# Two of the four token tiles of the dilated heads' v are accumulated in the retention's PSUM banks

## The chip, the cores and the metric

The kernel runs on one core of a Trainium2 chip, as one launch. The metric is the device time of one execution in microseconds. A core has five engines that run side by side, each through its own list of instructions in a fixed order: PE (matrix products, with the loads of its weights, PEld, beside them), DVE, ACT and POOL (element by element work) and SP, which here only issues DMAs. Matrix products are accumulated in PSUM, which has eight banks of 128 x 512 fp32; before a bank can take the next product, what stands in it has to be read out ("evacuated") by ACT or DVE.

## The reference

Two layers on 512 tokens of width 1024, in fp32. Each layer adds to x an attention part with three kinds of heads that all come from one projection of the normalised x, and then an MLP with squared relu. Cut to what matters:

```
def hybrid_layer(x, ...):
    h = rms_norm(x, attn_norm_w)
    ret_cols, dsa_cols, dil_cols = split(h @ w_in)
    mixed = concat([retention_mixer(ret_cols),    # 4 heads, chunks of 128, gated
                    dsa_mixer(dsa_cols),          # 4 heads, each query sees its 128 best keys
                    dilated_mixer(dil_cols)])     # 8 heads, three patterns of window and stride
    x = x + mixed @ w_out
    h = rms_norm(x, mlp_norm_w)
    return x + square(relu(h @ w_up)) @ w_down

def dsa_mixer(cols):
    q, c_kv, q_idx, k_idx, w_idx = split(cols)
    # the indexer: 8 small heads score all keys, and the 128 best of each query are kept
    logits = einsum('bqhd,bsd->bqhs', q_idx, k_idx)
    score = einsum('bqhs,bqh->bqs', relu(logits), w_idx)
    idx = top_k(where(causal, score, -inf), 128)
    return softmax(q . k[idx]) . v[idx]

def dilated_mixer(cols):
    q, k, v = split(cols)          # 8 heads of 64 columns each
    outs = [dilated_branch(q, k, v, window, dilation) for window, dilation in DIL_PATTERNS]
    return sum(softmax(lses) * outs)
```

The change is about v of the dilated heads: h times 512 columns of w_in.

## The kernel before

**Products.** Every fp32 operand is split into two halves of a rounded format, hi and lo, and every product is made of three matmuls (hi hi, hi lo, lo hi). A projection over 1024 rows is thus a group of 24 matmuls into one PSUM bank. `wform` (L336) puts weight columns on the partitions and all 512 tokens along the row (128x512); `tform` (L348) puts 128 tokens on the partitions and the columns along the row (128x256 for v). The splits of the weights ("w" in the rows) are made by ACT (hi, L278) and by POOL or DVE (lo, L286), some groups ahead.

**PSUM.** The eight banks are three pools: `mm` with 2 banks for the projections, `at` with 4 for attention scores and their products, and `rt` with 2. The `rt` banks are used by the retention, in the second half of a layer's attention, and by the down projection of the MLP. A pool gives its banks in turn, so a group of matmuls in `mm` starts only when the group two before it has been evacuated. A name such as mm_163_839 in the rows is the 839th tile to be made, of pool `mm`.

**The attention of a layer.** It begins with the stages of `ORD`, 'tv idx top dv0':

- tv: token parts (retention's v, the latent and the indexer's keys).
- idx, the indexer: for each pair of its 8 heads a projection of q, evacuated by ACT (L420) and DVE (L421); scores on PE into `at` (L443 and L444); a relu on ACT (L586) into a buffer P; a weighted sum on DVE (L591). A mask follows (L593).
- top: 16 rounds of MAX (L602) and MATCH_REPLACE (L603) on DVE, on three score tiles (512, 384 and 256 wide) each, and then the bias (L607).
- dv0: `dil_v` for heads 0 to 3. For each of 4 token tiles t, 24 matmuls of 128x256 (L348), and `evac_v`: a copy of the bank on ACT (L520), a hi cast of it on ACT (L524), and the subtraction for lo on POOL (L526), which reads the copy and not the bank.

Then come the heads, with "fill" work beside them: the projections q (L423 on ACT, L424 on DVE) and k (L436 on ACT, L438 on DVE) of further heads, `dil_v` for heads 4 to 7 (dv1, fill 'd'), the gates (L644 on ACT, L645 on DVE), the retention's q and k (L620, L623), and the retention itself (L657 to L733). A softmax head needs transposes on PE (L352), their copies by ACT (L485) and DVE (L486), and products with v (L491). At the end mixed @ w_out is added to x (L828).

**What sets the order.** The code is recorded once, and a scheduler (`schedule_with_timeline_sim=True`) then sets the order of each engine's instructions, by a simulated timeline and by the priorities of the table `PR`. So a stage later in the code can stand ahead of an earlier one: it depends on when the scheduler holds its operands and its bank to be free. On the chip each engine runs its list strictly in that order, and waits where an operand or a bank isn't there.

Of the kernel before, what the change touches and what calls it, by code (L numbers as in the profile page):

```python
# [123 lines left out]
class Kern:  # L124
# [412 lines left out]
    def dil_v(self, L, act, g):  # L537
        us = [(self.unit((L, "dv", g, k)), (k, k + 1, k + 2, k + 3)) for k in (0, 4)]
        for t in range(NT):
            ps = self.mm()  # L540
            self.tform(us, act, t, ps, 256)
            self.evac_dil(ps[:, 0:256], g, t)
        self.done(2)
# [586 lines left out]
```

## Time and profile before

| | us |
|---|---|
| median of 3 runs | 1255.89 (1255.29 to 1259.02) |
| the profiled execution | 1252.02 |
| its span in the trace | 1250.0 |
| attention of layer 0, about | 20 to 301 |
| MLP of layer 0, about | 301 to 620 |
| attention of layer 1, about | 635 to 915 |

The rows below come from the trace of that one execution; times in them count from the start of the span. Layer 1 repeats layer 0 some 615 us later. In the windows, "busy" of PE counts a matmul up to its modelled end, and PEld is the load of weights, which lies beside the matmuls. An idle time in a timeline stands in brackets behind the instruction that ended it, with the instruction that released it. PEclk is the granted clock of PE: 1.00 is 2.4 GHz, 0.5 is 1.2 GHz.

### The profile page before, as it was taken

How to read it: one execution, taken by the hardware profiler on the slowest of the kernel's cores; microseconds unless marked ns; L12 is line 12 of the kernel's file. 1: busy time of each engine (PE TensorE's matmuls, PEld its weight loads, DVE VectorE, ACT ScalarE, POOL GpSimd, SP SyncE). 2: the span in 40 equal slices, each digit the busy share in tenths (PEclk: the TensorE clock that was granted, in tenths of full speed). 3: DMA queues.
4: the chain of work that ended last, by engine and by line, in shares of the span. 5: the costliest groups of instructions: out<-in, count | busy, mean ns of one | idle time of the engine just before them, and what ended most of it. 6: DMA issues, size and time to landing. Idle time of an engine off the chain costs nothing.

```text
span 1250.0 us, 16890 instructions
## 1 busy us (share of the span) xinstructions
PE 1216.8 (97%) x6116; PEld 1031.2 (82%) x6116; DVE 915.4 (73%) x1582; ACT 680.1 (54%) x1241; POOL 474.7 (38%) x461
## 2 busy tenths in 40 slices
PE   7999999989999999999999999999899999999997
PEld 5987888878888888888889888878798888888886
DVE  6599757856785875857866996586769759577596
ACT  6646658734644535445556466586465445454454
POOL 3443648543411403204224545665534032041232
PEclk9999999999999999999999999999999999999999
DMA  7423223224435052151054332241170531514301
GB/s 214 119 72 106 68 69 119 69 67 120 150 103 152 16 186 84 64 171 31 21 164 114 93 84 85 69 124 45 51 250 21 183 87 56 180 35 135 84 1 68
DMA packets 142180, 122.73 MB, mean 98 GB/s; under 512 B 6801, under 2 KB 114065, under 8 KB 142098
## 3 DMA queue, kind: packets, MB, share of 16 engines
q1 hardware_dynamic: 140178, 118.52, 31.5%
q10 hardware_dynamic: 1920, 3.15, 1.0%
q8 instruction: 48, 0.79, 0.3%
q14 instruction: 34, 0.28, 0.1%
HBM read 114.31 MB, written 4.19 MB: 95 GB/s over the span
## 4 chain that ended last, share of the span: by engine, by line
PE 83%; DVE 13%; ACT 2%; issue 1%; DMA 0%; SPq 0%; POOL 0%; POOLq 0%; DVEq 0%; ACTq 0%
PE mm L336 34%; PE mm L348 15%; PE rt L1036 14%; PE at L1036 7%; DVE sc L603 3%; PE mm L1036 3%; DVE top L602 3%; PE at L352 2%; PE at L491 2%; PE at L443 1%; PE at L444 1%; PE at L336 1%; DVE ph L462 1%; PE rt L690 1%; DVE Q L424 1%
## 5 line engine op out<-in xcount | busy, mean ns | idle before, releaser
L336 PE MATMUL mm<-act,w 128*128 128x512 f32 (+2 forms) x2352 | 514.5, 377 | 1.4 <-DVE Q L424 1.4
L336 PEld LDWEIGHTS mm<-act,w 128*128 128x128 f32 x2352 | 424.2, 188 | 78.3 <-PE at L352 1.8
L286 POOL TENSOR_TENSOR w<-raw,w 128x512 fp32r<-128x512 f32 (+1 forms) x124 | 159.6, 1310 | 85.0 <-ACT w L278 70.0
L278 ACT CAST w<-raw 128x1024 fp32r<-128x1024 f32 (+1 forms) x138 | 142.8, 1037 | 81.2 <-PE rt L1036 27.6
L1036 PE MATMUL rt<-w,U 128*128 128x512 f32 x768 | 183.2, 389 | 0.0
L286 DVE TENSOR_TENSOR w<-rd,w 128x1024 fp32r<-128x1024 f32 x112 | 144.8, 1304 | 50.0 <-ACT w L278 50.0
L286 DVE TENSOR_TENSOR w<-raw,w 128x1024 fp32r<-128x1024 f32 (+1 forms) x76 | 94.4, 1243 | 106.2 <-ACT w L278 105.9
L1036 PEld LDWEIGHTS rt<-w,U 128*128 128x128 f32 x768 | 144.2, 188 | 29.9
L993 POOL TENSOR_TENSOR st<-s 128x256 f32<-128x256 f32 x32 | 39.1, 1222 | 330.1 <-ACT s L982 325.3
L278 ACT CAST w<-rd 128x1024 fp32r<-128x1024 f32 x112 | 117.6, 1050 | 83.4 <-PE rt L1036 41.7
L348 PE MATMUL mm<-w,act 128*128 128x256 f32 (+2 forms) x768 | 142.7, 336 | 5.6 <-ACT xv L524 3.1
L348 PEld LDWEIGHTS mm<-w,act 128*128 128x128 f32 x768 | 119.4, 191 | 18.7 <-ACT xv L524 3.6
L348 PE MATMUL mm<-w,mix 128*128 128x512 f32 x384 | 99.4, 406 | 1.6 <-DVE Q L424 1.1
L1036 PE MATMUL at<-w,U 128*128 128x512 f32 (+1 forms) x396 | 97.7, 386 | 0.0
L304 DVE TENSOR_TENSOR rd<-rd,rd 128x1024 f32<-128x1024 f32 x64 | 94.3, 1473 | 0.6
L1036 PEld LDWEIGHTS at<-w,U 128*128 128x128 f32 x396 | 73.6, 188 | 15.0
L348 PEld LDWEIGHTS mm<-w,mix 128*128 128x128 f32 x384 | 71.5, 193 | 16.3 <-PE rt L352 1.5
L980 ACT ACTIVATE s<-mm 128x512 f32<-128x512 f32 x62 | 36.9, 595 | 84.8 <-PE mm L336 75.1
L997 ACT CAST U<-st 128x1024 fp32r<-128x1024 f32 x32 | 33.7, 1054 | 80.9 <-POOL st L994 80.9
L991 POOL TENSOR_TENSOR st<-s,s 128x256 f32<-128x256 f32 x32 | 36.6, 1145 | 92.0 <-ACT s L982 92.0
L998 DVE TENSOR_TENSOR U<-s,U 128x256 fp32r<-128x256 f32 x64 | 63.8, 997 | 0.0
L463 ACT ACTIVATE ph<-ph,sm 128x128 f32<-128x128 f32 (+1 forms) x96 | 53.9, 562 | 16.8 <-DVE sm L462 16.0
(165 smaller groups left out, 1712.6 us busy)
## 6 DMA issues: line engine op xcount, KB each, us to landing
raw<-in_w_up_dram SPq DMA_DIRECT2D x64, 512.0 KB, 4.4
rd<-in_w_down_dram SPq DMA_DIRECT2D x32, 1024.0 KB, 5.1
raw<-in_w_in_dram SPq DMA_DIRECT2D x48, 512.0 KB, 3.9
raw<-in_w_out_dram SPq DMA_DIRECT2D x16, 512.0 KB, 3.8
xv<-in_x_dram SPq DMA_DIRECT2D x7, 512.0 KB, 4.9
KH<-KH ACTq DMA_DIRECT2D x24, 128.0 KB, 2.3
raw<-in_w_in_dram SPq DMA_DIRECT2D x8, 256.0 KB, 2.9
xd<-xv SPq DMA_DIRECT2D x4, 512.0 KB, 3.1
```

What stands on the lines that cost most here:

```text
L278: self.nc.scalar.copy(hi, src)
L286: eng.tensor_tensor(lo[:, i:i + step], src[:, i:i + step], hi[:, i:i + step].bitcast(F32), op=ALU.subtract)
L304: sub = lambda o, a, b: self.nc.vector.tensor_tensor(o, a, b, op=ALU.subtract)
L336: self.nc.tensor.matmul(ps[:cols, toks[0]:toks[1]], a, b, start=(k == 0 and j == 0), stop=(k == KB - 1 and j == 2))
L348: self.nc.tensor.matmul(ps[:, :w], a, b, start=(n == 0), stop=(n == tot - 1))
L463: nc.scalar.activation(p, p, AF.Exp, bias=a, scale=-1.0, accum_out=b)
L602: nc.vector.max(m, sc[b])
L603: nc.vector.match_replace(sc[b], m, sc[b], SENT)
L980: nc.scalar.activation(s, ps, AF.Relu)
L993: tt(st[:, 2], a[:, 0], a[:, 1], op=ALU.subtract)
L998: nc.vector.tensor_tensor(lo, src, hi.bitcast(F32), op=ALU.subtract)
L1036: nc.tensor.matmul(ps[:, c0:c1], a, w, start=(new and n == 0), stop=(n == 11), skip_group_check=True)
```

## The change

In `dil_v`, token tiles 0 and 1 still go to `mm` and tiles 2 and 3 go to `rt`. `dil_v` is called twice in each layer, as dv0 and as dv1. No instruction is added or removed.

```diff
--- before.py
+++ after.py
@@ -537,7 +537,7 @@
     def dil_v(self, L, act, g):
         us = [(self.unit((L, "dv", g, k)), (k, k + 1, k + 2, k + 3)) for k in (0, 4)]
         for t in range(NT):
-            ps = self.mm()
+            ps = self.mm() if t < 2 else self.rt_bank()
             self.tform(us, act, t, ps, 256)
             self.evac_dil(ps[:, 0:256], g, t)
         self.done(2)
```

Since the scheduler now has other banks for these tiles, it writes another order on all engines from the first attention stages of each layer to near its end; from about 280 us on, and in the MLP, the order of PE is as before. The two layers change alike.

The first place is on PE in the stage idx, at the scores at_101 of the indexer; mm_123 and mm_139 are its projections, w_78 and w_92 are the weights of dv0, mm_163/rt_163 is its tile 2 and mm_166/rt_166 its tile 3. Before:

```order
L443 MATMUL at_99_528<-KH_87_474,Q_94_511 128x256
L444 MATMUL at_99_528<-KH_87_474,Q_94_511 128x256
L443 MATMUL at_101_534<-KH_87_474,Q_94_511 128x512
L444 MATMUL at_101_534<-KH_87_474,Q_94_511 128x512
L336 MATMUL mm_123_624<-act_16_146,w_74_428 128x384 x6
L336 MATMUL mm_139_696<-act_13_143,w_76_433 128x384 x6
L336 MATMUL mm_139_696<-act_14_144,w_76_433 128x384 x6
```

And now:

```order
L443 MATMUL at_101_534<-KH_87_474,Q_94_511 128x512
L444 MATMUL at_101_534<-KH_87_474,Q_94_511 128x512
L336 MATMUL mm_123_624<-act_15_145,w_74_428 128x384 x2
L336 MATMUL mm_123_624<-act_16_146,w_74_428 128x384 x6
L348 MATMUL rt_163_839<-w_78_438,act_13_143 128x256 x3
L348 MATMUL rt_163_839<-w_78_438,act_14_144 128x256 x2
L336 MATMUL mm_139_696<-act_13_143,w_76_433 128x384 x5
L443 MATMUL at_103_540<-KH_87_474,Q_94_511 128x384
L444 MATMUL at_103_540<-KH_87_474,Q_94_511 128x384
```

Five matmuls of dv0's tile 2 now stand among the first projections and scores of the indexer, where there was none.

The second place is on PE at the indexer's last score, at_153; mm_173 is the projection of q for the first head. Before:

```order
L443 MATMUL at_153_762<-KH_87_474,Q_142_727 128x256
L444 MATMUL at_153_762<-KH_87_474,Q_142_727 128x256
L348 MATMUL mm_163_839<-w_78_438,act_13_143 128x256 x6
L348 MATMUL mm_163_839<-w_78_438,act_14_144 128x256 x6
L348 MATMUL mm_163_839<-w_92_505,act_15_145 128x256 x6
L348 MATMUL mm_163_839<-w_92_505,act_16_146 128x256 x6
L348 MATMUL mm_166_869<-w_78_438,act_13_143 128x256 x6
L348 MATMUL mm_166_869<-w_78_438,act_14_144 128x256 x6
L348 MATMUL mm_166_869<-w_92_505,act_15_145 128x256 x6
L348 MATMUL mm_166_869<-w_92_505,act_16_146 128x256 x6
L336 MATMUL mm_173_911<-act_13_143,w_108_577 128x512 x6
```

And now:

```order
L348 MATMUL mm_161_810<-w_92_505,act_16_146 128x256 x4
L443 MATMUL at_153_762<-KH_87_474,Q_142_727 128x256
L444 MATMUL at_153_762<-KH_87_474,Q_142_727 128x256
L348 MATMUL mm_161_810<-w_92_505,act_16_146 128x256
L348 MATMUL rt_166_869<-w_78_438,act_13_143 128x256 x4
L348 MATMUL rt_166_869<-w_78_438,act_14_144 128x256 x6
L348 MATMUL rt_166_869<-w_92_505,act_15_145 128x256 x6
L348 MATMUL rt_166_869<-w_92_505,act_16_146 128x256 x6
L336 MATMUL mm_173_911<-act_13_143,w_108_577 128x512 x6
```

Before, 48 of dv0's 96 matmuls stood behind the last score, in two banks of `mm`; now 73 stand ahead of it, and 22 of those behind it are in `rt`.

The third place is on DVE, in the top-k, at the evacuation of mm_173 (L424). Before:

```order
L602 MAX top3_241_1347<-sc3_90_479 128x8
L602 MAX top2_242_1350<-sc2_89_478 128x8
L602 MAX top1_243_1353<-sc1_88_477 128x8
L603 MATCH_REPLACE sc3_90_479<-top3_241_1347,sc3_90_479 128x512
L603 MATCH_REPLACE sc2_89_478<-top2_242_1350,sc2_89_478 128x384
L603 MATCH_REPLACE sc1_88_477<-top1_243_1353,sc1_88_477 128x256
L602 MAX top3_244_1356<-sc3_90_479 128x8
L424 SCALAR_TENSOR_TENSOR Q_176_942<-mm_173_911,Q_176_942 64x512
```

And now:

```order
L602 MAX top1_192_1056<-sc1_88_477 128x8
L603 MATCH_REPLACE sc2_89_478<-top2_191_1053,sc2_89_478 128x384
L603 MATCH_REPLACE sc3_90_479<-top3_238_1338,sc3_90_479 128x512
L603 MATCH_REPLACE sc1_88_477<-top1_192_1056,sc1_88_477 128x256
L602 MAX top2_239_1341<-sc2_89_478 128x8
L602 MAX top3_241_1347<-sc3_90_479 128x8
L602 MAX top1_240_1344<-sc1_88_477 128x8
L424 SCALAR_TENSOR_TENSOR Q_176_942<-mm_173_911,Q_176_942 64x512
```

Before, 13 MAX and 12 MATCH_REPLACE stood between the indexer's last sum and this evacuation; now it is 9 and 7.

The fourth place is on PE at mm_206, a projection of k; w_187 and w_199 are the weights of dv1, and rt_260 and rt_263 its tiles 2 and 3. Before:

```order
L491 MATMUL at_212_1202<-PT_214_1208,xv_159_805 128x512
L352 MATMUL at_215_1213<-cst_85,ph_181_985 128x128 x4
L352 MATMUL at_217_1225<-cst_85,ph_181_985 128x128 x2
L336 MATMUL mm_206_1162<-act_13_143,w_174_936 128x512 x6
L336 MATMUL mm_206_1162<-act_14_144,w_174_936 128x512 x6
L336 MATMUL mm_206_1162<-act_15_145,w_174_936 128x512 x6
L336 MATMUL mm_206_1162<-act_16_146,w_174_936 128x512 x5
L491 MATMUL at_212_1202<-PT_214_1208,xv_159_805 128x512
L336 MATMUL mm_206_1162<-act_16_146,w_174_936 128x512
```

And now:

```order
L491 MATMUL at_212_1202<-PT_214_1208,xv_159_805 128x512
L352 MATMUL at_215_1213<-cst_85,ph_181_985 128x128 x4
L352 MATMUL at_217_1225<-cst_85,ph_181_985 128x128 x2
L348 MATMUL rt_260_1462<-w_199_1113,act_15_145 128x256 x5
L491 MATMUL at_212_1202<-PT_214_1208,xv_159_805 128x512
L348 MATMUL rt_260_1462<-w_199_1113,act_16_146 128x256 x6
L348 MATMUL rt_263_1492<-w_199_1113,act_15_145 128x256 x5
L348 MATMUL rt_263_1492<-w_199_1113,act_16_146 128x256 x6
L336 MATMUL mm_206_1162<-act_13_143,w_174_936 128x512 x5
L491 MATMUL at_212_1202<-PT_216_1218,xv_159_805 128x384
```

48 of dv1's 96 matmuls, which stood some way behind mm_206, now stand ahead of it.

How many MAX and MATCH_REPLACE stand on DVE ahead of an instruction (of 96 in all), and its place in DVE's list, for the second of each pair of evacuations:

| instruction on DVE | before | after |
|---|---|---|
| L424 of mm_173 | 29, place 106 | 21, place 98 |
| L424 of mm_198 (the bank that mm_206 takes next) | 55, place 159 | 51, place 157 |
| L438 of mm_202 | 63, place 171 | 59, place 169 |
| L438 of mm_206 (the bank that mm_255, tile 0 of dv1, takes next) | 69, place 186 | 73, place 197 |
| L645 of mm_226 | 76, place 200 | 77, place 203 |

## Rows read from the trace of the kernel before

**Rows 1.** The page, busy times and the chain that ended last (line by engine)

```profile
PE 1216.8 (97%) x6116; PEld 1031.2 (82%) x6116; DVE 915.4 (73%) x1582; ACT 680.1 (54%) x1241; POOL 474.7 (38%) x461
...
PE 83%; DVE 13%; ACT 2%; issue 1%; DMA 0%; SPq 0%; POOL 0%; POOLq 0%; DVEq 0%; ACTq 0%
```

**Rows 2.** Windows of layer 0: us, busy us per engine, PEclk, DMA share, GB/s

```profile
60.00:73.00 13.00, 10.58 (x75) 9.56 (x73) 11.94 (x19) 8.54 (x21) 2.72 (x3) 1.00 0.16 43
...
80.00:146.00 66.00, 64.49 (x351) 55.19 (x350) 65.18 (x198) 37.63 (x79) 34.78 (x36) 1.00 0.34 93
146.00:190.00 44.00, 44.00 (x223) 36.95 (x222) 20.77 (x62) 24.06 (x53) 22.58 (x27) 1.00 0.25 72
...
276.00:284.00 8.00, 8.00 (x28) 6.81 (x27) 4.17 (x10) 1.87 (x6) 3.87 (x5) 0.57 0.00 1
```

**Rows 3.** Timeline of PE, 58 to 80: start, us, instructions [idle before, releaser]

```profile
60.42 2.86 PE L348 MATMUL mm<-w,act 128*128 128x256 f32 x22 [0.28 <-DVE Q L421]
...
65.60 0.44 PE L443 MATMUL at<-KH,Q 128*128 128x384 f32 x1 [0.57 <-ACT P L586]
...
71.12 0.28 PE L444 MATMUL at<-KH,Q 128*128 128x256 f32 x1
72.97 6.01 PE L348 MATMUL mm<-w,act 128*128 128x256 f32 x48 [1.57 <-ACT xv L524]
78.82 1.55 PE L336 MATMUL mm<-act,w 128*128 128x512 f32 x6
```

**Rows 4.** Timeline of PE, 106 to 131

```profile
109.88 0.51 PE L491 MATMUL at<-PT,xv 128*128 128x512 f32 x1 [0.27 <-ACT PT L485]
...
111.72 5.49 PE L336 MATMUL mm<-act,w 128*128 128x512 f32 x23 [0.68 <-DVE Q L424]
...
125.39 3.12 PE L348 MATMUL mm<-w,act 128*128 128x256 f32 x24
...
129.95 1.33 PE L348 MATMUL mm<-w,act 128*128 128x256 f32 x9 [0.54 <-DVE P L645]
```

**Rows 5.** Waits of PE in 632 to 920 (layer 1): total us, times, longest

```profile
PE mm L348 <- ACT xv L524: 1.6, 1, 1.6
...
PE mm L336 <- DVE Q L424: 0.7, 1, 0.7
...
PE at L443 <- ACT P L586: 0.6, 1, 0.6
PE mm L348 <- DVE P L645: 0.5, 1, 0.5
```

**Rows 6.** Chain of waits, 60 to 100: start, us, what

```profile
73.77 1.38 DVE top L602 x3
75.15 1.58 DVE sc L603 x3
```

**Rows 7.** Timeline of DVE, 69 to 75 and 116 to 126

```profile
69.61 3.55 DVE L591 SCALAR_TENSOR_TENSOR sc<-P,widx,sc 128x512 f32<-128x512 f32 x6 [0.20 <-ACT P L586]
...
123.34 0.69 DVE L438 TENSOR_TENSOR KL<-mm,KH 64x512 fp32r<-64x512 f32 x1
```

**Rows 8.** Timeline of DVE, 143 to 154

```profile
143.96 1.64 DVE L607 TENSOR_SCALAR sc<-sc 128x384 f32<-128x384 f32 x2
...
147.51 0.69 DVE L645 SCALAR_TENSOR_TENSOR P<-P,mm 128x512 f32<-128x512 f32 x1 [1.18 <-ACT P L644]
148.93 0.69 DVE L486 TENSOR_TENSOR PT<-at,PT 128x512 fp32r<-128x512 f32 x1 [0.73 <-ACT PT L485]
153.17 0.68 DVE L438 TENSOR_TENSOR KL<-mm,KH 64x512 fp32r<-64x512 f32 x1 [3.55 <-ACT KH L436]
```

**Rows 9.** Timeline of POOL, 36 to 50

```profile
42.03 5.25 POOL L286 TENSOR_TENSOR w<-raw,w 128x512 fp32r<-128x512 f32 x4 [0.35 <-ACT w L278]
```

**Rows 10.** Timeline of PE, 190 to 196

```profile
191.33 0.60 PE L352 MATMUL rt<-cst,mix 128*128 128x128 f32 x4
```

**Rows 11.** Windows of layer 1, as Rows 2

```profile
890.00:896.00 6.00, 6.00 (x33) 5.20 (x33) 3.18 (x6) 2.14 (x6) 2.82 (x4) 0.72 0.02 3
```


## The prediction

> **What bounds the kernel now.** I read the page's busy times and chain first. PE is busy 1216.8 us of the 1250.0 us span, and it carries 83% of the chain that ended last, DVE 13% [rows 1]. So time can only be won where PE waits, or where its clock is low, and the sum below goes by PE's idle time alone. DVE's 13% has to lie in one stretch, and the windows show which: from 60 to 73 us DVE is busy 11.94 of 13.00 us and PE 10.58; from 80 to 146 DVE is busy 65.18 of 66.00 and PE 64.49; from 146 to 190 PE is busy 44.00 of 44.00 and DVE 20.77 of 44 [rows 2]. The middle one is the top-k, one MAX and MATCH_REPLACE after the other (1.38 + 1.58 us for a round of all three score tiles) [rows 6]. Both engines are nearly full there, so I must ask of each PE wait that goes whether DVE lets PE run ahead.
>
> Then PE's timeline, for the single waits. In the indexer there are three: 0.28 us for DVE's Q (L421), 0.57 us for a relu (L586), and 1.57 us, just before the 48 matmuls of dv0's tiles 2 and 3, for ACT's cast xv (L524) [rows 3]. The last is the wait for a bank that the change is about: tile 2 wants the `mm` bank that tile 0 still holds, and ACT reads that one out late. Sum 0.28 + 0.57 + 1.57 = 2.42 us, and the window has 13.00 - 10.58 = 2.42 too [rows 2]. In the top-k there are three more: 0.27, 0.68 and 0.54 us, in all 1.49, for PT (L485), for Q (L424) and for the gate's product (L645) [rows 4]. Layer 1 has the same: 1.6, 0.6, 0.7 and 0.5 us by the same lines [rows 5].
>
> **The change, part by part.** Nothing is added, so each term is a wait that goes or comes. (1) *The bank.* With tiles 2 and 3 in `rt` no matmul of dv0 waits for L524 of tile 0. The two `rt` banks are idle there: the next use of them, by the retention, is at 191.33 us [rows 10], long after the evacuation of dv1 too. An L348 matmul takes (78.82 - 72.97)/48 = 0.122 us [rows 3]; I hold it to be the same into `rt`. Gain 1.57.
>
> (2) *Filler in the indexer.* 5 of dv0's matmuls now stand ahead of the third row of scores, and in all 73 instead of 48 ahead of the last score. PE's other two waits there were for a bank (L421) and for at (L586), which come at a given time of DVE and ACT; PE now comes to them later, by up to 25 x 0.122 = 3.05 us, so 0.28 and 0.57 go. The weights must be ready earlier: their lo halves on POOL run from 42.03 to 47.28 [rows 9], and the first such matmul stands at the scores of at_101, which PE comes to after that. Sum of (1) and (2): 2.42.
>
> (3) *The price of (2).* The last score comes later by 3.05 - 0.28 - 0.57 = 2.2 us at most, and with it the last sums on DVE (six of them from 69.61 on, [rows 7]) and the start of the top-k. On DVE that is a delay of 0 to 2.2 us for all that stands in the top-k, less what is moved ahead. It has room at the end: L607 ends at 143.96 + 1.64 = 145.6, and then DVE waits 1.18, 0.73 and 3.55 us for ACT [rows 8], while PE waits for nothing up to 190 [rows 2]. So the delay itself costs nothing if PE gets its banks.
>
> (4) *Waits in the top-k.* For mm_173 DVE's queue is 8 half-rounds shorter, for mm_198 and mm_202 4 each; a half-round, one MAX or MATCH_REPLACE, takes (1.38 + 1.58)/6 = 0.49 us [rows 6]. So these evacuations come 2 to 4 us earlier in the queue, which outweighs the later start of 0 to 2.2. Moreover 48 matmuls of dv1 now stand ahead of mm_206, 48 x 0.122 = 5.9 us in which PE doesn't need that bank. The waits of 0.27, 0.68 and 0.54 us go: 1.49.
>
> (5) *A new wait.* L438 of mm_206 is at place 197 of DVE instead of 186. DVE does an instruction in 65.18/198 = 0.33 us there [rows 2], so it ends 11 x 0.33 = 3.6 us later, and up to 2.2 more by (3): 123.34 + 0.69 + 3.6 = 127.6 to 129.8 us [rows 7]. The matmuls that want its bank, dv1's tile 0, began at 125.39 [rows 4]; PE now comes to them 5.9 us later by (4) and 2.42 + 0.27 + 0.68 = 3.4 us earlier by the waits gone, at 127.9. So PE waits 0 to 1.9 us. I take 0.7, near the lower end, since DVE's last sums were themselves not the last thing to wait for a score: DVE still had a backlog when the last one came, at 71.12 + 0.28, and ended the sums at 73.16 [rows 3, 7]. Queued behind that matmul is all of PE; ACT and DVE have other work then.
>
> (6) *The end of the attention.* PE's list differs there in a few places, with waits under a microsecond each. From 276 to 284 us the granted clock is 0.57, between its two levels of 1.2 and 2.4 GHz, which costs (1 - 0.57) x 8 = 3.4 us [rows 2]; in layer 1 it is 0.72 for 6 us, 1.7 us [rows 11]. It follows a thin stretch of PE that the change hardly touches. I put (6) at nothing, with bounds of -5.1 (no drop in either layer) and +5.1 (twice the drop).
>
> Sum for a layer: 2.42 + 1.49 - 0.7 = 3.2 us, for two 6.4 us. The profiled execution took 1252.02 us, 2.02 around its span, so I expect 1252.0 - 6.4 = 1245.6 for its like. It lies 3.87 under the median of the runs shown, 1255.89, against which the forecast is measured: 1255.9 - 6.4 = **1249.5 us**. Own range: both layers at their best, 2 x 3.91 = 7.8, and no clock drop, 5.1, give 1243.0; the new wait at its dearest, 2 x (3.91 - 1.9) = 4.0, and a clock drop half as long again, 2.6, give 1254.5.
>
> **The rivals.** *No change: DVE sets the pace.* From 60 to 146 us DVE is busier than PE. If PE's lead is given back at each evacuation, waits of the same sum show up at other L424 and L438 lines, and the time is 1255.9. For it: DVE's 65.18 of 66.00 us [rows 2]. Against it: DVE waits 5.46 us right after the top-k while PE waits for nothing, so the top-k ends with room [rows 8]. Beside it, the Trainium skill ("Perfetto Trace Analysis", Identifying the Most-Contended Engine) takes the engine with the highest occupancy as the one to optimise first, and judges TensorE by the busy share of its weight loads. By it DVE bounds the top-k (99% against PEld's 84%), and a change that only relieves PE brings nothing there. The Trainium skill also says that a gap which repeats on the busy engine can mean too few buffers ("Perfetto Trace Analysis", Optimization Strategy); the 1.57 us gap agrees, but comes once in a layer.
>
> The Trainium skill also has a measurement against the change: "TensorE: Matmul & The Clock Gate", HAM oscillation, tells of a kernel with its loop made contiguous to which double-buffering in PSUM gave no further gain (126.6 to 125.5 us). By that the sum would be about nothing; here the trace names a wait for a bank, which the Trainium skill doesn't show of that kernel.
>
> *Slower: the later last score is what counts.* The place is the start of the top-k, behind 25 more matmuls. If the retention's inputs, the heads' evacuations and the softmaxes all hang on DVE, its 2.2 us of delay in each layer go into the time: 1255.9 + 2 x 2.2 = 1260.3. This decides if DVE's L607 ends over 1.18 + 0.73 = 1.9 us later than now against PE's other work, so that PE waits between 146 and 160, where it has no idle time now. For it: DVE has no other slack between 60 and 146 than 0.82 + 1.06 us [rows 2]. Against it: 3.55 us of wait follow [rows 8].
>
> *The clock.* With nothing else won, a clock drop gone gives 1255.9 - 5.1 = 1250.8, one doubled 1261.0. Nothing in the rows speaks for either.
>
> **How the numbers follow.** The forecast's mechanism (waits gone, most of the lead kept) 0.60; DVE gives the pace and takes it back, 0.25; slower through the top-k, 0.15, each with the clock's play in it. 0.3% of the time, 3.8 us, is about what a measurement of this kernel can tell from no change. Of the forecast's 0.60, 0.54 lie beyond it and 0.06 within; of the 0.25, 0.19 within and 0.03 to each side; of the 0.15, 0.12 slower and 0.03 within. So faster 0.57, same 0.28, slower 0.15. The range goes from 1244, a little above the best case, to 1260, which holds the case of no change and most of the slower one.
>
> **What would show it.** Right, step by step: (1) no wait for L524 near 71 us, and L348 rows into `rt` from the first scores on; (2) PE without idle time from 60 to 80; (3) top-k starting 0 to 2.2 us after 73.77 and L607 ending by 148, with shorter DVE waits behind it; (4) no waits for L424 and L645 in the top-k; (5) one wait of under 1.9 us for L438 at an L348 into `mm`, at about 128 us; (6) a clock of about 0.57 and 0.72 at the ends of the attention. It is wrong if PE's idle sum from 60 to 146 is still near 3.9 us under other names, if PE waits between 146 and 190, or if an L348 into `rt` waits for a split of w (L286).

## The result, and the profile after

| | before | after |
|---|---|---|
| median, us | 1255.59 (1253.34 to 1259.02, 4 runs) | 1238.22 (1236.08 to 1238.82, 4 runs) |
| ratio | | 0.9854 (95%: 0.9829 to 0.9878) |
| the profiled execution, us | 1252.02 | 1236.08 |
| its span, us | 1250.0 | 1234.1 |

The kernel is 17.4 us faster by the medians, where 6.4 was forecast, and the time lies below the range of 1244 to 1260. The two profiled executions differ by 15.9 us, and that is what has to be found. The granted clock alone doesn't make it: in one series of 23 executions of before those with a mean granted clock of 0.994 to 0.996 took 1252.56 to 1255.99 us and those at 0.991 and 0.992 took 1257.06 to 1259.42, while after, at 0.994 to 0.997, took 1236.08 to 1238.82.

The page of after, to be read against [rows 1]: busy times, and the chain by engine.

```profile
PE 1207.2 (98%) x6116; PEld 1027.6 (83%) x6116; DVE 921.4 (75%) x1582; ACT 679.2 (55%) x1241; POOL 472.4 (38%) x461
...
PE 85%; DVE 12%; ACT 1%; issue 1%; DMA 1%; SPq 0%; POOL 0%; POOLq 0%; DVEq 0%; ACTq 0%
```

PE is busy for 9.6 us less, with the same 6116 matmuls, and DVE for 6.0 us more. So busy times don't tell where the time went. The windows of after, over the same stretches as [rows 2], and one of the end of layer 1's attention (us, busy us of PE, PEld, DVE, ACT, POOL with counts, PEclk, DMA share, GB/s):

```profile
60.00:73.00 13.00, 13.00 (x99) 12.64 (x98) 11.85 (x19) 8.53 (x19) 2.86 (x2) 1.00 0.16 43
...
80.00:146.00 66.00, 63.56 (x349) 54.58 (x348) 65.13 (x202) 37.97 (x80) 32.38 (x33) 1.00 0.34 94
146.00:190.00 44.00, 43.69 (x229) 37.15 (x228) 23.78 (x69) 25.98 (x57) 24.94 (x30) 1.00 0.27 78
...
276.00:284.00 8.00, 8.00 (x43) 6.65 (x42) 5.88 (x13) 3.32 (x11) 3.89 (x4) 1.00 0.00 0
...
872.00:890.00 18.00, 16.79 (x84) 14.06 (x83) 13.43 (x28) 6.80 (x19) 7.97 (x10) 0.91 0.06 19
```

From 60 to 73 us PE has no idle time left (13.00 of 13.00, it was 10.58), from 80 to 146 it has more of it than before (63.56 busy, it was 64.49). The clock drop at 276 us is gone in layer 0, and layer 1 has one of (1 - 0.91) x 18 = 1.6 us, about as before (1.7 [rows 11]). None of this makes 15.9 us. What finds it is holding the starts of the same instructions of PE against each other. These are the starts of eight groups in before: transposes in the first stage, the retention's transposes of its second, third and fourth tile, the MLP's first projection, and in layer 1 the retention's first, second and fourth tile (its first of layer 0 stands in [rows 10]):

```profile
21.51 0.60 PE L352 MATMUL at<-cst,KH 128*128 128x128 f32 x4
...
218.71 0.60 PE L352 MATMUL rt<-cst,mix 128*128 128x128 f32 x4
...
246.03 0.60 PE L352 MATMUL rt<-cst,mix 128*128 128x128 f32 x4
...
272.33 0.60 PE L352 MATMUL rt<-cst,mix 128*128 128x128 f32 x4
...
300.68 4.55 PE L336 MATMUL mm<-act,w 128*128 128x256 f32 x36
...
806.78 0.60 PE L352 MATMUL rt<-cst,mix 128*128 128x128 f32 x4
...
834.09 0.60 PE L352 MATMUL rt<-cst,mix 128*128 128x128 f32 x4
...
887.66 0.60 PE L352 MATMUL rt<-cst,mix 128*128 128x128 f32 x4
```

And in after, the same with the retention's first tile of layer 0:

```profile
21.09 0.60 PE L352 MATMUL at<-cst,KH 128*128 128x128 f32 x4
...
188.18 0.60 PE L352 MATMUL rt<-cst,mix 128*128 128x128 f32 x4
...
215.44 0.60 PE L352 MATMUL rt<-cst,mix 128*128 128x128 f32 x4
...
241.02 0.60 PE L352 MATMUL rt<-cst,mix 128*128 128x128 f32 x4
...
265.34 0.60 PE L352 MATMUL rt<-cst,mix 128*128 128x128 f32 x4
...
291.04 5.99 PE L336 MATMUL mm<-act,w 128*128 128x256 f32 x48
...
794.48 0.60 PE L352 MATMUL rt<-cst,mix 128*128 128x128 f32 x4
...
821.73 0.60 PE L352 MATMUL rt<-cst,mix 128*128 128x128 f32 x4
...
871.61 0.60 PE L352 MATMUL rt<-cst,mix 128*128 128x128 f32 x4
```

Between two such rows PE does the same matmuls in both kernels (151 from the retention's first to its second tile, 286 in B), in another order. The differences, with A for what stands ahead of the retention, B from its second to its fourth tile, and C from there to the MLP:

| stretch of PE | before | after | saved |
|---|---|---|---|
| to the first stage's transposes | 21.51 | 21.09 | 0.42 |
| A, layer 0 (to the retention's first tile) | 169.82 | 167.09 | 2.73 |
| first to second tile | 27.38 | 27.26 | 0.12 |
| B, layer 0 | 53.62 | 49.90 | 3.72 |
| C, layer 0 | 28.35 | 25.70 | 2.65 |
| MLP of layer 0 and A of layer 1 | 506.10 | 503.44 | 2.66 |
| first to second tile | 27.31 | 27.25 | 0.06 |
| B, layer 1 | 53.57 | 49.88 | 3.69 |
| from there to the end of the span | 362.3 | 362.5 | -0.2 |

So 5.6 us lie where the forecast looked for 6.4, in and right behind A. 7.4 us lie in B, which the forecast put at nothing, and 2.65 in C of layer 0, where the clock drop is gone. The 0.42 us of the first row are not the change's: up to there the order of every engine is the same.

**Stretch A.** PE in after, at the last score of the indexer and in the top-k, and the second half of the evacuation of mm_173 on DVE:

```profile
72.37 0.28 PE L444 MATMUL at<-KH,Q 128*128 128x256 f32 x1
72.49 0.28 PE L348 MATMUL mm<-w,act 128*128 128x256 f32 x1
72.61 2.80 PE L348 MATMUL rt<-w,act 128*128 128x256 f32 x22
75.25 6.99 PE L336 MATMUL mm<-act,w 128*128 128x512 f32 x30
...
87.89 5.70 PE L336 MATMUL mm<-act,w 128*128 128x512 f32 x24 [1.57 <-DVE Q L424]
...
129.93 3.10 PE L348 MATMUL mm<-w,act 128*128 128x256 f32 x24 [0.61 <-DVE KL L438]
```

```profile
87.05 0.69 DVE L424 SCALAR_TENSOR_TENSOR Q<-mm,Q 64x512 fp32r<-64x512 f32 x1
```

The same evacuation in before, and the matmuls of PE that take that bank next:

```profile
89.07 0.69 DVE L424 SCALAR_TENSOR_TENSOR Q<-mm,Q 64x512 fp32r<-64x512 f32 x1
```

```profile
89.91 5.69 PE L336 MATMUL mm<-act,w 128*128 128x512 f32 x24
```

The 22 matmuls of dv0's tile 3 follow the last score without a wait, into `rt`. The first projection for the heads starts at 75.25 instead of 78.82 [rows 3], 3.15 us earlier beside the 0.42. That is more than the 2.42 in brackets, since a bracket doesn't hold all that a wait costs: in [rows 3] the L444 at 71.12 was followed by the next matmul after 1.85 us, in after the like one at 72.37 after 0.12, so the wait of 1.57 us cost 1.73. By the same measure the other two, 0.28 and 0.57 in brackets, cost 0.44 and 0.74. Then DVE takes part of the lead back: at 87.89 PE waits 1.57 us for L424 of mm_173, where before shows no wait. But before had nothing to spare there: its matmuls start at 89.91, 0.15 us after that L424 ended (89.07 + 0.69), and those of after just the same (87.05 + 0.69, and 87.89). PE came 3.6 us earlier (3.15 and 0.42), L424 only 2.0, and PE goes on with the 2.0. The forecast new wait for L438 is there, 0.61 us at 129.93.

**Stretch B.** Its 286 matmuls are the same ones in both kernels. Of the 3.7 us, 1.7 lie between the second and the third tile (27.32 and 25.58 us) and 2.0 between the third and the fourth (26.30 and 24.32). But 11 matmuls have moved from the first part into the second: 157 and 129 in before, 146 and 140 in after. So the second part does more in less time, and the place to look is there. These are windows of before, first 13.3 us and then the 7.76 up to the end of the last head's work:

```profile
251.00:264.30 13.30, 13.30 (x78) 11.16 (x78) 3.90 (x8) 3.85 (x8) 4.78 (x6) 1.00 0.08 23
264.30:272.06 7.76, 5.82 (x29) 4.05 (x28) 7.54 (x18) 3.69 (x8) 4.87 (x5) 1.00 0.73 197
```

DVE is busy for 3.90 of 13.30 us and then for 7.54 of 7.76, and PE is full in the first window and starved in the second: 5.82 of 7.76 by its matmuls, 4.05 by its weight loads. The same distances ahead of the fourth tile in after:

```profile
244.01:257.31 13.30, 13.30 (x83) 11.33 (x82) 7.92 (x21) 7.13 (x16) 3.27 (x5) 1.00 0.24 80
257.31:265.07 7.76, 7.76 (x44) 6.52 (x42) 7.40 (x13) 3.81 (x8) 6.83 (x6) 1.00 0.26 75
```

DVE's work is spread (7.92 of 13.30), and PE has 7.76 of 7.76. The DMA share, 0.73 in before's starved window and 0.26 here, doesn't explain it: the same instructions take as long in both (L348 on PE 404 and 395 ns, L486 on DVE 678 and 686 for 512 columns). What DVE waited for in before, and the waits of PE that followed (DVE first, then PE):

```profile
263.82 0.86 DVE L709 TENSOR_REDUCE rw<-rt 64x128 f32<-64x256 f32 x2 [3.82 <-PE rt L699]
```

```profile
265.42 0.38 PE L491 MATMUL at<-PT,vs 128*128 128x256 f32 x1 [0.82 <-ACT PT L485]
...
270.80 1.30 PE L491 MATMUL at<-PT,vs 128*128 128x384 f32 x5 [0.46 <-DVE PT L486]
```

L709 is the retention's reduction over its third tile. It waits 3.82 us for L699 on PE, and with it come all the retention's other sums, just when the last head needs its copies (L486, L485). In after the same L709:

```profile
254.52 0.86 DVE L709 TENSOR_REDUCE rw<-rt 64x128 f32<-64x256 f32 x2 [0.97 <-PE at L352]
```

L709 starts at 254.52 there, 13.5 us behind the third tile's transposes (241.02), in before 17.8 behind them (246.03). In before the scheduler had put products of the output projection between those of the retention:

```order
L348 MATMUL mm_563_3062<-w_459_2525,mix_172_910 128x512 x6
L348 MATMUL mm_563_3062<-w_503_2770,mix_516_2843 128x512 x2
L690 MATMUL rt_490_2685<-sv_62_301,rT_447_2442 128x256
L699 MATMUL rt_492_2701<-rv_445_2434,rw_491_2698 128x256 x2
L348 MATMUL mm_563_3062<-w_503_2770,mix_516_2843 128x512
L699 MATMUL rt_492_2701<-rv_445_2434,rw_491_2698 128x256
L348 MATMUL mm_558_3036<-w_425_2338,mix_418_2302 128x512
```

In after the three L699 stand together, right behind the last L690, and the output projection's products stand later, between the last head's transposes and its products with v.

### The profile page after: what moved, and what is told of

Read it like the earlier page. It is cut to its first block, busy times and chain, and to the rows that moved or that the text cites. A ratio compares the mean times of both kernels' runs of the same rounds, so it can differ in the third digit from the quotient of the medians.

```text
span 1234.1 us, 16904 instructions
## 1 busy us (share of the span) xinstructions
PE 1207.2 (98%) x6116; PEld 1027.6 (83%) x6116; DVE 921.4 (75%) x1582; ACT 679.2 (55%) x1241; POOL 472.4 (38%) x461
## 3 DMA queue, kind: packets, MB, share of 16 engines
q10 hardware_dynamic: 1920, 3.15, 1.0%
## 4 chain that ended last, share of the span: by engine, by line
PE 85%; DVE 12%; ACT 1%; issue 1%; DMA 1%; SPq 0%; POOL 0%; POOLq 0%; DVEq 0%; ACTq 0%
PE mm L336 35%; PE mm L348 15%; PE rt L1036 14%; PE at L1036 7%; PE mm L1036 3%; DVE sc L603 3%; DVE top L602 3%; PE at L352 2%; PE at L491 2%; PE at L444 1%; PE at L443 1%; DVE ph L462 1%; PE at L336 1%; DVE Q L424 1%; DMA raw<-in_w_in_dram 1%
## 5 line engine op out<-in xcount | busy, mean ns | idle before, releaser
L348 PE MATMUL mm<-w,act 128*128 128x456 f32 (+2 forms) x576 | 118.4, 351 | 3.0 <-DVE act L400 1.8
L348 PEld LDWEIGHTS mm<-w,act 128*128 128x128 f32 x576 | 96.4, 189 | 15.2 <-DVE act L400 2.8
L348 PE MATMUL mm<-w,mix 128*128 128x512 f32 x384 | 97.3, 401 | 0.6 <-DVE Q L424 0.5
L348 PEld LDWEIGHTS mm<-w,mix 128*128 128x128 f32 x384 | 70.5, 190 | 15.2 <-DVE Q L424 0.9
```

The source lines that it names most:

```text
L348: self.nc.tensor.matmul(ps[:, :w], a, b, start=(n == 0), stop=(n == tot - 1))
```

## The experiments

Two questions were open: whether the order of B makes its length (ORDER below), or the banks do (BANKS), or PE's earlier arrival (EARLY), or the clock (CLOCK); and what of the order it is (SPLIT or FILLER). Each run leaves the computation as it is.

**Tiles in rt in dv0 alone.**

```diff
-            ps = self.mm() if t < 2 else self.rt_bank()
+            ps = self.mm() if g or t < 2 else self.rt_bank()
```

> Tiles 2 and 3 go to rt only in dv0 (heads 0 to 3), so the wait for L524 at the start of the top-k goes, but the order of PE in the retention's part of the attention is nearly that of before. Stretch A is from the start of the span to the retention's first transposes (191.33 us before, 188.18 after), stretch B from the retention's second transposes to its fourth (218.71 to 272.33 = 53.6 us before, 215.44 to 265.34 = 49.9 after). Theory ORDER (the 3.7 us a layer that the forecast missed come from the order in stretch B, and not from the banks): A like after, 188 to 189; B like before, 53 to 54; time 4 to 8 us under before, 1248 to 1252. Rival EARLY (B got shorter since PE reaches it earlier, the bank of dv0 is the cause of all): B about 50, time 12 to 18 us under before. Rival CLOCK (what was missed is the drop of the granted clock at the end of the attention): B like before, but 276 to 284 at a clock of 1.00, and 7 to 11 us under before.

Measured: 1252.52 us, ratio to before 0.9977 (0.9963 to 0.9991). The retention's second and fourth tile on PE:

```profile
217.51 0.60 PE L352 MATMUL rt<-cst,mix 128*128 128x128 f32 x4
...
271.12 0.60 PE L352 MATMUL rt<-cst,mix 128*128 128x128 f32 x4
```

B is 53.61 us, as in before: ORDER, and not EARLY. Nor CLOCK: the drop behind B is there. The time lies just above the 1248 to 1252 that was expected, and A, expected at 188 to 189, ends at 190.12; in layer 1 nothing of a lead is left (506.13 us for the MLP and A, before 506.10). The lead is there at first and is given back, at PT (L485) and at the gate's product (L645):

```profile
108.06 0.50 PE L491 MATMUL at<-PT,xv 128*128 128x512 f32 x1 [1.45 <-ACT PT L485]
...
129.60 3.01 PE L348 MATMUL mm<-w,act 128*128 128x256 f32 x23 [1.08 <-DVE P L645]
```

**Tiles in rt in dv1 alone.**

```diff
-            ps = self.mm() if t < 2 else self.rt_bank()
+            ps = self.mm() if not g or t < 2 else self.rt_bank()
```

> Tiles 2 and 3 go to rt only in dv1 (heads 4 to 7). dv0's tile 2 still takes its bank from tile 0, so the wait for L524 (1.6 us a layer) can stay; the order of PE in stretch B is nearly that of after. Theory ORDER: A within 1.5 us of before (190 to 192), B like after, 50 us, in both layers, so 7 to 10 us under before, 1246 to 1249. Rival EARLY: A and B as before, within 0.3% of before. Rival CLOCK: B as before, the only gain is a clock drop that is gone, 3 to 5 us.

Measured: 1244.58 us, ratio 0.9909 (0.9889 to 0.9929). A ends at 191.42, B is 49.87 (218.68 to 268.55) and 49.89 in layer 1, with the clock drop still at its end. Without any gain in A the kernel has 11 us by the medians, a little more than the 7 to 10 that were expected. So dv0's bank, on which the forecast rested, is the smaller part.

**Odd tiles in rt; tiles 2 and 3 in at.**

```diff
-            ps = self.mm() if t < 2 else self.rt_bank()
+            ps = self.rt_bank() if t % 2 else self.mm()
```

> Tiles 1 and 3 (not 2 and 3) go to rt, in dv0 and dv1. The order of PE in stretch B is the same as in after, instruction by instruction; that ahead of it differs in a few places. Theory ORDER: B 50 us, time within 4 us of after (1235 to 1242). Rival EARLY: the time depends on A alone, which is then within 1.5 us of after; B between 50 and 54 as A is. Rival CLOCK: B 53 to 54 us.

Measured: 1235.25 us, ratio 0.9835 (0.9814 to 0.9856); A 188.45, B 49.90 (215.69 to 265.59). It is the lowest median of all, but its interval overlaps that of after.

```diff
-            ps = self.mm() if t < 2 else self.rt_bank()
+            ps = self.mm() if t < 2 else self.at()
```

> Tiles 2 and 3 go to the four banks of at, not to rt, in dv0 and dv1. The order of PE in stretch B is the same as in before, instruction by instruction; the wait for tile 0's bank goes, but the scores of the indexer now share their banks with dv0. Theory ORDER: B 53 to 54 us as before, so a gain of A alone, 0 to 7 us under before (1248 to 1256). Rival EARLY: B shorter by what A is shorter, 12 to 18 us under before if A is like after. Rival CLOCK: B as before, and the time goes by the clock at the end of the attention, 3 to 8 us under before.

Measured: 1254.82 us, ratio 0.9990 (0.9975 to 1.0005); A 191.69, B 53.59 (219.01 to 272.60). The wait for tile 0's bank is gone there too, and nothing is left of it at 190 us. In all four runs B is 49.9 or 53.6, and it goes with the order: in both layers PE, DVE, ACT and POOL each have in B the order of before, instruction by instruction, with dv0 alone and with `at`, and that of after with dv1 alone and with the odd tiles. But all that had the new order, after among them, had dv1 in `rt` too, so BANKS was left as a rival.

**The banks of after with the end of before; the banks of before with an end like after's.**

```diff
- 'stage_dv0': -50
+ 'stage_dv0': -150      (banks of after)
```

> The banks of after (tiles 2 and 3 of dv0 and dv1 in rt), with one priority changed (stage_dv0 from -50 to -150), by which the scheduler writes the end of the attention, stretch B and behind, exactly in the order of before; the order ahead of the retention is near that of after. Theory ORDER: B 53 to 54 us in both layers as in before, so some 7 us over after, 1243 to 1249. Rival BANKS (it is dv1 in rt that shortens B, the order only goes with it): B 50 us, and the time within 0.3% of after. Of the two reasons for a B of 50 in the runs so far, dv1 in rt and the order, this run has the first alone.

Measured: 1251.49 us, ratio to before 0.9966 (0.9953 to 0.9979): most of the gain is lost, more than the 7 us of B, and the time lies above the 1243 to 1249 that were expected. The second and fourth tile, and the two windows as above:

```profile
217.81 0.60 PE L352 MATMUL rt<-cst,mix 128*128 128x128 f32 x4
...
271.42 0.60 PE L352 MATMUL rt<-cst,mix 128*128 128x128 f32 x4
```

```profile
250.10:263.40 13.30, 13.30 (x79) 11.17 (x78) 3.90 (x8) 3.87 (x8) 4.80 (x6) 1.00 0.07 20
263.40:271.10 7.70, 5.77 (x28) 4.04 (x27) 7.53 (x18) 3.69 (x8) 4.86 (x5) 1.00 0.70 198
```

B is 53.61 with dv0 and dv1 in `rt`, and DVE is idle and then late as in before (3.90 of 13.30, 7.53 of 7.70). All four engines have the order of before in B and from there to the MLP. BANKS falls. A ends at 190.40 instead of 188.18. The priority also moved dv0, and the clock falls in A:

```profile
89.78 7.32 PE L336 MATMUL mm<-act,w 128*128 128x512 f32 x24 [2.21 <-DVE Q L424]
```

These 24 matmuls take 7.32 us, in after 5.70; the granted clock is 0.76 from 89 to 96 us. In layer 1, without such a drop, the MLP and A take 504.97 us, 1.5 more than in after.

```diff
- 'hi_o': -20
+ 'hi_o': -70            (banks of before)
```

> The banks of before (all of dv0 and dv1 in mm), with one priority changed (hi_o from -20 to -70, that of the hi cast of the output projection's weights). PE's order is that of before up to 190 us, word for word, and at the end of the attention like after's in what matters to the theory: 9 products of the output projection stand between the transposes of the last head and its products with v. Theory ORDER: A 191 to 192 us as before, B 49 to 51 us in both layers, so 5 to 9 us under before, 1246 to 1250 (with a clock drop as in before). Rival BANKS: B 53 to 54 us, time within 0.3% of before.

Measured: 1255.05 us, ratio 0.9999 (0.9987 to 1.0012). The first, second and fourth tile, and two waits of PE between the first two:

```profile
190.77 0.60 PE L352 MATMUL rt<-cst,mix 128*128 128x128 f32 x4
...
222.06 0.60 PE L352 MATMUL rt<-cst,mix 128*128 128x128 f32 x4
...
271.77 0.60 PE L352 MATMUL rt<-cst,mix 128*128 128x128 f32 x4
```

```profile
209.93 0.44 PE L491 MATMUL at<-PT,xv 128*128 128x384 f32 x1 [1.47 <-ACT PT L485]
210.95 0.39 PE L443 MATMUL at<-KH,Q 128*128 128x256 f32 x1 [0.58 <-DVE sm L462]
```

B is 49.71, with all of dv in `mm` and an order nearer to after's than to before's: a B near 50 needs no tile in `rt`, so ORDER again. The time was missed. The same priority also wrote another order for the 151 matmuls from the first to the second tile, with new waits, and behind these the granted clock is 0.57 from 212 to 216 us. They take 31.29 us instead of 27.38, which eats what B gains.

```diff
- 'hi_o': -20
+ 'hi_o': -70            (banks as with the odd tiles)
```

> The odd tiles in rt, as in the run of that name, with hi_o at -70, which writes a third order in stretch B that is like neither of the two (a tenth to a third of the matmuls stand elsewhere). Theory ORDER: A as with the odd tiles, 188.5 us within 0.5; B has a value of its own between 48 and 54 us, and the time moves with twice the difference of B to 49.9. Rival BANKS: B 49.9 us as with the odd tiles, and the same time within 0.3%.

Measured: 1252.91 us, ratio 0.9985 (0.9970 to 0.9999); A 189.02, B 54.33 (219.37 to 273.70) and, in layer 1, 51.58. A third order and other lengths, but they can't be held against 49.9 and 53.6 as they stand: 2 more matmuls stand in B in layer 0, 7 fewer in layer 1, and in layer 0 the granted clock is 0.76 from 223 to 230 us. It is 17.7 us behind the odd tiles by the medians, where twice the difference of B would have been 9: this expectation was missed too. From the first to the second tile PE takes 30.35 us, with 8 matmuls fewer, instead of 27.24. What the run shows is that the banks of the faster kernel are no gain in themselves.

**What of the order it is.**

```diff
- 'ret_9': -20
+ 'ret_9': -820          (banks of before)
```

> The banks of before, and PE's order of before but for one place in each layer (ret_9 from -20 to -820): 9 products of the output projection that stand among the last products of the retention's third tile (L690, L699) stand behind them. By the windows of before, DVE waits 3.8 us for that L699 at 263.8 and then has more to do than PE can wait for. Theory SPLIT (stretch B is long since the retention's products are split by others, so that DVE is idle first and late afterwards): L699 ends 9 x 0.227 = 2.0 us earlier, DVE goes on 2 us earlier, and B falls from 53.6 to 51.5 to 52.5 us, 2 to 4 us off the time (0.2 to 0.3%). Rival FILLER (what counts is only that 9 products stand between the last head's transposes and its products with v, which they don't here): B 53.3 to 53.7, time within 0.1% of before.

Measured: 1252.30 us, ratio 0.9977 (0.9961 to 0.9994). The second and fourth tile, and L709 on DVE:

```profile
221.52 0.60 PE L352 MATMUL rt<-cst,mix 128*128 128x128 f32 x4
...
273.95 0.60 PE L352 MATMUL rt<-cst,mix 128*128 128x128 f32 x4
```

```profile
264.52 0.86 DVE L709 TENSOR_REDUCE rw<-rt 64x128 f32<-64x256 f32 x2 [1.72 <-PE rt L699]
```

DVE's wait falls from 3.82 to 1.72 us and B from 53.62 to 52.43, as SPLIT has it and FILLER doesn't: 1.2 us a layer for nine matmuls put behind the last of the retention's products. All of it lies between the third and the fourth tile (25.11 us instead of 26.30, with the same 129 matmuls).

```diff
- 'hs_9': 400
+ 'hs_9': 300            (banks of before)
```

> The banks of before, with hs_9 at 300 instead of 400, by which the last products of the retention's third tile stand together as in after (18 matmuls from first to last, 29 before), and other matmuls of stretch B stand elsewhere too. Theory SPLIT: B 50 to 52 us. Rival FILLER: B by how many products stand behind the last head's transposes, of which there are 9 here as well, so 50 to 52 too: this run tells the two apart from BANKS alone, by which B is 53.6.

Measured in one execution: 1252.29 us; B 51.49 (221.38 to 272.87) and 51.51 in layer 1. Some 0.5 us of the difference to 53.6 are 5 matmuls that stand ahead of B here. That speaks against BANKS once more, and doesn't tell SPLIT from FILLER; the run before did. Of the 3.7 us a layer the split of the retention's products is 1.2; the rest goes with the other moves in B, the 11 matmuls brought into its second part among them, which were not taken apart.

## Why the prediction was wrong

- *Terms (1) and (2), the bank and the filler: right, 2.42 forecast and 3.15 measured.* The size was read from brackets, and a bracket holds less than a wait costs (0.28, 0.57 and 1.57 cost 0.44, 0.74 and 1.73 us).
- *Term (3), the later top-k: right.* The last L607 ends at 146.8, by 148 as forecast. PE has 0.31 us of idle time from 146 to 190, which the prediction named as a sign of being wrong; but this wait for L623 stands in before too, at 192.24, just behind the window.
- *Term (4), waits in the top-k: wrong.* Waits of 0.27, 0.68 and 0.54 us went, but one of 1.57 for L424 came at mm_173's bank. Its place in DVE's list had moved up by 8 half-rounds, 3.9 us in the prediction's terms, and was held against DVE's later start alone. In the end L424 came 2.0 us earlier and PE 3.6. A place in a queue has to be held against the lead of the engine that waits, for the first evacuation as for the last, and a bank without a wait can still be free only just in time (0.15 us behind L424 in before).
- *Term (5), the new wait for L438: right,* 0.7 forecast and 0.61 measured, at 129.93 (forecast, about 128). That the terms come to 2.7 us in A of each layer, with 3.2 forecast, is in part luck: (1) and (2) were too small and (4) too large.
- *Term (6), the end of the attention: this is the step that failed.* "PE's list differs there in a few places, with waits under a microsecond each", and it was put at nothing, with bounds from the clock alone; the prediction saw "a thin stretch of PE" there, but held that "the change hardly touches" it. B saved 3.7 us in each layer, 7.4 in all, which by itself takes the forecast of 1249.5 to 1242.1, below the range. The places were not few: at most 219 of B's 286 matmuls stand in the same sequence in both kernels, and 80 of DVE's 100 instructions. The waits under a microsecond were the visible end of a long one: from 264.3 to 272.06 PE's weight loads are busy for 4.05 of 7.76 us. The window beside it, with DVE at 3.90 of 13.30, would have told that DVE had been starved just before. Both views were of the trace of before. A size was to be had: at the 84% of the window beside it (11.16 of 13.30), PE's 4.05 us of loads fit in 4.8 us, so some 2.9 of the 7.76 us were free. The part from the third to the fourth tile, in which this window lies, got 2.0 us shorter and took in 11 more matmuls.
- *The clock.* The drop of layer 0 is gone in the profiled execution of after, 2.65 us in C; that of layer 1 is not. The range had this as a part of its lower end. That the change took the drop away isn't shown: it doesn't go with the order of the instructions (last section).
- *The rivals.* That DVE takes PE's lead back is what happens with dv0 alone in `rt` and with both in `at`. From the first stage's transposes on, A of layer 0 is 0.95 us shorter with dv0 alone, 0.9 longer with `at`, 0.2 longer with dv1 alone, and 2.73 shorter with both in `rt`; the MLP and A of layer 1 are 0.03 longer, 0.7 longer, 0.07 shorter and 2.66 shorter. Runs that have PE's order of before there take up to 1.1 us (A) and 1.6 us (the MLP and A) longer than before does, so what each alone brings can't be told from nothing; what both bring can. My reading, argued from the waits of these runs and not tested: dv0 gives the lead, and dv1's 48 matmuls are what PE does while DVE is late. That they are free of `mm` isn't enough: with `at` they are too, but the scheduler doesn't put them there.

The Trainium skill's rule from "Perfetto Trace Analysis", Identifying the Most-Contended Engine, that weight loads and not matmuls show how far TensorE is from its limit, was used for the top-k alone. At the end of B it tells the story: in before matmuls are busy for 5.82 of 7.76 us, weight loads for 4.05.

The scheduler wrote the shorter B by its own simulated timeline. Which of its times tipped it was not tried, and nothing in the change speaks for B: dv1 alone, or the odd tiles, give the new order, `at` and dv0 alone the old one.

## What to carry to other kernels

Where a scheduler writes the order, a change of a buffer is a change of all orders behind it, and the gain or loss may lie 150 us from the edit. Lay the two orders beside each other to the end, and for each stretch that differs set as its bound what PE's weight loads leave free there, not the sum of the waits in brackets. Two windows in a row in which first one engine and then the other is idle mark work that can be interleaved. An engine's lead was kept here only where it had other work at the places at which the slower one handed something over; so two changes can be worth little alone and more together.

## What was not expected of the hardware

The clock drop at the end of layer 0's attention, 0.57 from 276 to 284 us in before, followed the stretch in which PE was starved, and in after that stretch is full and the drop is gone. But layer 1 has the same order in after, no starved stretch either, and PEclk 0.91 from 872 to 890. The other runs say the same: with dv1 alone B is as full as in after (49.87 us) and the drop is there as in before; with `at` B and C have the order of before on all four engines, and the drop is half of before's:

```profile
272.00:280.00 8.00, 8.00 (x29) 6.80 (x28) 4.63 (x10) 2.14 (x6) 3.84 (x5) 0.57 0.00 1
```

```profile
276.00:284.00 8.00, 8.00 (x35) 6.82 (x35) 5.09 (x12) 2.26 (x7) 3.94 (x6) 0.79 0.00 1
```

So neither the starved stretch nor the order alone decides it, and no run here tells what does.

What a drop cost was less than its share. C, 132 matmuls, is 25.70 us in after and 25.72 with the odd tiles, both without a drop. It is 26.75 with `at`, where (1 - 0.79) x 8 = 1.7 us of clock were lost, 28.35 in before with 3.4 lost, and 29.85 in the run with ret_9 at -820, where the clock was 0.53 from 276 to 287 and 5.2 were lost. The cost is 1.05, 2.65 and 4.15 us, some 0.6 to 1.1 less than the loss each time.
